# Rotated attention queries on all 128 partitions, padded with zeros

## The chip, the cores and the metric

The kernel runs on one core of one Trainium2 chip. The metric is the device time of one execution in microseconds (us); lower is better. TensorE (PE in the profile; PEld is its weight load, which can overlap the products) multiplies, VectorE (DVE) and ScalarE (ACT) work elementwise, GpSimd (POOL) here only fills tiles and copies a few columns, and SyncE (SP) issues most transfers.

## The reference

Two blocks of a network run over 256 tokens of width 2048, all in float32: gated linear attention with a convolution and a feed-forward, then a pooling mixer, then a multi-head attention layer. The change lies in the attention layer. It has 16 heads; the query and the key of a head have 192 values, of which 128 are plain and 64 are rotated by position. The rotated 64 of the key are the same for all heads up to a factor for each head and token.

```python
QBLOCK, N_HEADS, QK_NOPE, QK_ROPE, V_HEAD = 128, 16, 128, 64, 128
def qk_norm_rope(t, g, cos, sin):
    t = rmsnorm(t, g)
    return jnp.concatenate([t[..., :QK_NOPE], apply_rope(t[..., QK_NOPE:], cos, sin)], axis=-1)
def chunk_causal_attention(q, k, v):
    ...
    for i in range(S // QBLOCK):
        q0, k_end = i * QBLOCK, (i + 1) * QBLOCK
        s = jnp.einsum('bqhd,bkhd->bhqk', q[:, q0:k_end], k[:, :k_end]) * scale
        ...
        p = jax.nn.softmax(s, axis=-1)
        outs.append(jnp.einsum('bhqk,bkhd->bqhd', p, v[:, :k_end]))
```

## The kernel before

Activations lie transposed: features on the 128 partitions, 256 tokens along the row. All weights stream from HBM once, in the order of `weight_order`, in blocks of 1 MB. Each block is worked as two halves, called half-blocks here (a "unit" in the code). For each half-block ACT rounds the weights to a high part `wh` (L225), DVE takes the rest `wl` (L193), and PE multiplies both with the activations, which are split the same way. `wh` and `wl` have four buffers each and are made three half-blocks ahead, so ACT may run ahead of PE until it needs the buffer that PE still reads. PE executes strictly in the order in which the program was written.

Everything else is written as generators ("tasks") that take a step after a half-block: evictions from PSUM, norms, rotations, the attention itself. A task goes on when its tiles are there, when a PSUM place is free (three places called main, two called misc), and for attention when at least six of the 33 big tiles in SBUF ("slots") are free. So the number of live tiles helps to decide after which half-block a step is written, on all engines.

In the last stage the task `attend(hq)` does four heads at once (hq from 0 to 3; "head group" below). It writes the scores of two blocks of 128 queries. The first block sees 128 keys, the second 256; each is one main PSUM place of four heads. The heads stand in the order 0, 2, 1, 3. For each head there are two float32 products into the same place: the plain part, with queries `qn` and keys `kn` on 128 partitions, and the rotated part, with `qr` and `krp`. Two heads share a tile of rotated values: the even head has partitions 0 to 63 and the odd one 64 to 127, so this product takes 64 rows of the array. In the trace a float32 product is two passes, each a weight load (LDWEIGHTS) and a MATMUL; "64\*128" in a row is a product on 64 rows, "128\*128" one on 128.

Then ACT copies the scores to SBUF (`s`), POOL masks a corner, DVE takes the maximum, ACT the exponential, DVE divides, PE transposes (misc<-cm,s), ACT copies to `pt0` and `pt1`, PE multiplies with the values (main<-pt,v), ACT copies the result (`oraw`), DVE multiplies with the gate, and ACT and DVE split it into the `part` tiles that the output projection (bout, the last 32 half-blocks) reads, one head group after another. `qn_steps` also sums squares over partitions, as sixteen passes with a single column (misc<-ones,sq).

`qr_steps` makes the rotated queries, two tiles of eight heads, by `rope_rows`: a product with a fixed matrix, two multiplications with cosine and sine and one addition.

Of the kernel before, what the change touches and what calls it, by code (L numbers as in the profile page):

```python
# [99 lines left out]
def kernel(  # L100
# [11 lines left out]
    nc = tc.nc  # L112
# [36 lines left out]
    def slot(name, shape=(P, 4, T), dt=F32):  # L149
        return Slot(spool, big_places, "slot", shape, dt, name)  # L150
# [34 lines left out]
    def elems(a):  # L185
        return math.prod(a.shape[1:])
# [4 lines left out]
    def tt(out, a, b, op):  # L191
        vec_cost(out)
        nc.vector.tensor_tensor(out, a, b, op)  # L193

    def mul(out, a, b):
        tt(out, a, b, ALU.mult)

    def add(out, a, b):
        tt(out, a, b, ALU.add)
# [27 lines left out]
    def mm(out, lhsT, rhs, start, stop):  # L227
        n = elems(rhs)
        spent["PE"] += (n / 2.4 if rhs.dtype == F32R else max(n / 0.6, 214.0)) + 2
        nc.tensor.matmul(out, lhsT, rhs, start=start, stop=stop, skip_group_check=True)  # L230
# [188 lines left out]
    def group_tok(name, g, rhs, kbs=range(NKB)):  # L419

        ps = psum_now("main", (P, 2, 512))
        kbs = list(kbs)
        for i, kb in enumerate(kbs):
            for half in range(2):
                wh, wl = next_unit(name, g, kb)
                x = rhs(i)[half]
                for j in range(2):
                    first = i == 0 and half + j == 0
                    last = i == len(kbs) - 1 and half + j == 2
                    for t in range(2):  # L430
                        tk = slice(t * P, (t + 1) * P)
                        mm(ps[:, t, :], x[:, j, 0, tk], wh[:, j, :], first, False)
                        mm(ps[:, t, :], x[:, j, 0, tk], wl[:, j, :], False, False)
                        mm(ps[:, t, :], x[:, j, 1, tk], wh[:, j, :], False, last)
                end_unit()
        return ps
# [393 lines left out]
    for g in range(4):  # L830
        ps = group_tok("v", g, h)
# [4 lines left out]
    for g in range(4):  # L836
        hold = {}
        ps = group("cc", g, h)
# [6 lines left out]
        ps = group("cx", g, h)  # L845
# [19 lines left out]
        ps = group("cb", g, h)  # L865
# [12 lines left out]
    for g in range(4):  # L878
        ps = group("gb", g, h)
        gt = {}  # L880
        spawn(gate_steps(ps, get("R"), AF.Sigmoid, gt, 0))
        ps = group("conv_out", g, cbu)
# [11 lines left out]
    for g in range(4):  # L894
        ps = group("r", g, h)
# [15 lines left out]
    for g in range(4):  # L911
        ps = group("ga", g, h)
# [4 lines left out]
        ps = group("gla_out", g, op)  # L917
# [24 lines left out]
    def residual(g):  # L942
        def into(ps, fs):
            for part in range(2):
                add(xs[g][:, fs, :], ps[:, :, part, :], xs[g][:, fs, :])

        return into
# [77 lines left out]
    for part in range(4):  # L1025
# [5 lines left out]
        for g in range(4):  # L1031
            ps = group("down", g, hid, range(4 * part, 4 * part + 4), residual(g))
# [49 lines left out]
    for half in range(2):  # L1082
        y = Pair(4)
        for gi in (2 * half, 2 * half + 1):
            pooled = Pair(2)
            for n in range(2):
                ps = group("u", 2 * gi + n, hp)
# [5 lines left out]
            for n in range(2):  # L1093
                ps = group("pgate", 2 * gi + n, hp)
# [3 lines left out]
            for n in range(2):  # L1098
                ps = group("pgroup", 2 * gi + n, pooled, range(2))
# [15 lines left out]
        for g in range(4):  # L1115
            ps = group("pout", g, y, range(4 * half, 4 * half + 4), residual(g))
# [52 lines left out]
        yield from rms_steps(s, 512, r, cc)  # L1169
        rows["R" + key], rows["C" + key] = r, cc  # L1170

    def rope_rows(out, raw, n):

        ps = yield from psum_later("misc", (P, n, T))
        mm(ps.t, rot, raw, True, True)
        mul(out, raw, wide(C, n))
        yield 1
        t = slot("rt", (P, n, T))
        mul(t.t, ps.t, wide(S, n))
        ps.done()  # L1180
        add(out, out, t.t)
        t.free()

    kro = row("kro")
# [30 lines left out]
    kn, krp, vq = [None] * 4, [None] * 2, []  # L1215
# [42 lines left out]
        rk.free()  # L1258
        kn[g] = k

    qn, qr, qr2 = [None] * 4, [None] * 2, [None] * 2
    qss, qsc = small("qss", (P, 2, 16)), small("qsc", (P, 2, 16))

    def qn_steps(g, ps):
# [25 lines left out]
    def qr_steps(g, ps):  # L1290
        raw, sq = slot("qraw"), slot("sq")
        act(raw.t, ps.t, AF.Copy, scale=col("q_rope"))
        act(sq.t, ps.t, AF.Square)
        ps.done()
        qr2[g] = sq
        yield 2
        s = slot("qr")
        for b in range(2):
            yield from rope_rows(s[:, 2 * b:2 * b + 2, :], raw[:, 2 * b:2 * b + 2, :], 2)
        raw.free()  # L1300
        qr[g] = s

    ob = Pair(4)
    begun = {}
    HEAD_AT = (0, 2, 1, 3)
    def attend(hq):
        while None in (qn[hq], kn[hq], qr[hq // 2], krp[hq // 2]):
            yield 1
        while hq and (hq - 1 not in begun or state["unit"] < begun[hq - 1] + STAGGER):
            yield 1  # L1310
        while len(big_places) < 6:
            yield 1
        begun[hq] = state["unit"]

        rq = rows["Cq"]
        hs = slice(4 * hq, 4 * hq + 4)
        a, b = qss[:, :, hs], qsc[:, :, hs]
        for t in range(2):
            r = rq[:, t:t + 1]
            ts(qss[:, t, hs], qss[:, t, hs], r, r, ALU.mult, ALU.mult)  # L1320
        yield from rstd_steps(b, a, lambda: ts(a, a, 1.0 / QK_HEAD, EPS, ALU.mult, ALU.add))
        for t in range(2):
            ts(qsc[:, t, hs], qsc[:, t, hs], rq[:, t:t + 1], QK_HEAD**-0.5, ALU.mult, ALU.mult)
        probs, mxs = [], []
        for blk in range(2):
            w = P * (blk + 1)
            ps = yield from psum_later("main", (P, 4, T))
            qsl = slice(blk * P, (blk + 1) * P)
            for c in range(4):
                i = HEAD_AT[c]  # L1330
                hd = 4 * hq + i
                bs = slice(64 * (hd % 2), 64 * (hd % 2) + 64)
                jr = hd // 2
                mm(ps[:, c, 0:w], qn[hq][:, i, qsl], kn[hq][:, i, 0:w], c % 2 == 0, False)
                mm(ps[:, c, 0:w], qr[jr // 4][bs, jr % 4, qsl], krp[jr // 4][bs, jr % 4, 0:w], False, True)
            yield 1
            s = slot("s")
            probs.append(s)
            act(s[:, :, 0:w], ps[:, :, 0:w], AF.Copy)
            ps.done()  # L1340
            nc.gpsimd.memset(s[0:64, :, w - 64:w], -1e30)
        qn[hq].free()
        kn[hq].free()
        yield 1
        for blk in range(2):
            w = P * (blk + 1)
            mx = small("mx", (P, 3, 4))
            mxs.append(mx)
            nc.vector.reduce_max(mx[:, 0, :], probs[blk][:, :, 0:w], axis=AX.X)
            stt(mx[:, 0, :].rearrange("p (b a) -> p b a", b=2), mx[:, 0, :].rearrange("p (b a) -> p b a", b=2),  # L1350
                -1.0, qsc[:, blk, hs].rearrange("p (a b) -> p b a", b=2), ALU.mult, ALU.mult)
        yield 1
        for blk in range(2):
            w = P * (blk + 1)
            mx = mxs[blk]
            for c in range(4):
                hd = 4 * hq + HEAD_AT[c]
                sv = probs[blk][:, c, 0:w]
                act(sv, sv, AF.Exp, scale=qsc[:, blk, hd:hd + 1], bias=mx[:, 0, c:c + 1],
                    accum_out=mx[:, 1, c:c + 1])  # L1360
        yield 2
        for blk in range(2):
            w = P * (blk + 1)
            nc.vector.reciprocal(mxs[blk][:, 2, :], mxs[blk][:, 1, :])
            for c in range(4):
                sv = probs[blk][:, c, 0:w]
                ts(sv, sv, mxs[blk][:, 2, c:c + 1], None, ALU.mult)
        yield 2
        pt0, pt1 = slot("pt0"), slot("pt1", (P, 4, P))
        for src, sc, dst in ((probs[0], slice(0, P), pt0[:, :, 0:P]), (probs[1], slice(0, P), pt0[:, :, P:T]),  # L1370
                             (probs[1], slice(P, T), pt1.t)):
            ps = yield from psum_later("misc", (P, 4, P))
            for c in range(4):
                nc.tensor.transpose(ps[:, HEAD_AT[c], :], src[:, c, sc], ident)  # L1374
            yield 1
            act(dst, ps.t, AF.Copy)
            ps.done()
        for s in probs:
            s.free()
        yield 2  # L1380
        while len(vq) <= hq:
            yield 1
        po = yield from psum_later("main", (P, 4, T))
        for i in range(4):
            isl = slice(i * P, (i + 1) * P)
            mm(po[:, i, :], vq[hq][:, 0, isl], pt0[:, i, :], i % 2 == 0, False)
            mm(po[:, i, P:T], vq[hq][:, 1, isl], pt1[:, i, :], False, True)
        vq[hq].free()
        pt0.free()
        pt1.free()  # L1390
        yield 1
        o = slot("oraw")
        act(o.t, po.t, AF.Copy)
        po.done()
        while hq not in gates:
            yield 1
        yield 1
        mul(o.t, o.t, gates[hq].t)
        gates[hq].free()
        ob.put(hq, o.t)  # L1400
        o.free()
# [4 lines left out]
    for i, (name, g) in enumerate(MLA):  # L1406
# [8 lines left out]
        else:  # L1415
            ps = group_tok(name, g, cl, [0])
# [134 lines left out]
```

## Time and profile before

| | |
|---|---|
| three runs | 2775.38, 2773.48, 2775.07 us; median 2775.07 us |
| profiled execution, its own time | 2773.71 us |
| its span, first to last instruction | 2771.9 us |
| busy: PE, PEld | 2759.3 us (100%), 2403.6 us (87%) |
| busy: DVE, ACT, POOL | 1787.4 us (64%), 1346.4 us (49%), 25.7 us (1%) |
| mean granted TensorE clock | 0.999 of full speed |

Busy time of PE is not PE at its peak: matmuls are pipelined, and a product that waits inside the engine for its weights counts as busy. So the distance between starts tells more than a duration. A share of the whole span says little on the attention, which takes the last 210 us or so; stretches of it have to be asked for. The granted clock is given as a share of 2.4 GHz, so 0.50 is the lower of the two levels, 1.2 GHz.

### The profile page before, as it was taken

To read this page: it belongs to the slowest core of one execution; us is meant where nothing else is said; L and a number is where in the kernel's file an instruction comes from. 1 tells how busy PE (TensorE), PEld (TensorE's weight loads), DVE (VectorE), ACT (ScalarE), POOL (GpSimd) and SP (SyncE) were. 2 spreads that over 40 slices of the span, in tenths; PEclk is the share of its full clock that TensorE was granted. 3 is DMA by queue.
4 is the path that set the end of the run, shared out by engine and by line. 5 is a ranking of instruction groups with operands and counts; after the bars stand their busy time and mean duration, and the time that the engine had idled before them with its cause. 6 is when DMAs were issued, how large, how long until landed. Compare 5 with 4: busy or idle time off the path is not lost.

```text
span 2771.9 us, 38593 instructions
## 1 busy us (share of the span) xinstructions
PE 2759.3 (100%) x15906; PEld 2403.6 (87%) x15906; DVE 1787.4 (64%) x2119; ACT 1346.4 (49%) x1584; POOL 25.7 (1%) x36
## 2 busy tenths in 40 slices
PE   8999999999999999999999999999999999999999
PEld 7888888888888888888888888888888888899788
DVE  6676666655665666656556566687657677768464
ACT  5644444444554444434444345554434445555563
POOL 0000000000000000000000000000000000000000
PEclk9999999999999999999999999999999999999999
DMA  6444455555555655555555555555555555555244
GB/s 250 175 149 155 167 182 183 194 186 189 191 182 198 214 193 186 185 195 183 194 185 191 189 185 195 190 185 195 185 193 185 186 194 199 201 181 183 92 171 148
DMA packets 73712, 511.69 MB, mean 185 GB/s; under 512 B 8208, under 2 KB 8752, under 8 KB 13248
## 3 DMA queue, kind: packets, MB, share of 16 engines
q1 hardware_dynamic: 72496, 506.94, 51.9%
q8 instruction: 124, 2.03, 0.3%
q10 hardware_dynamic: 1040, 2.29, 0.2%
q14 instruction: 52, 0.43, 0.0%
HBM read 504.99 MB, written 4.21 MB: 184 GB/s over the span
## 4 chain that ended last, share of the span: by engine, by line
PE 99%; DVE 0%; DMA 0%; ACT 0%; issue 0%; SPq 0%; DVEq 0%; ACTq 0%
PE main L230 96%; PE misc L230 2%; DMA raw<-w_q_dram 0%; PE misc L1374 0%; DVE wl L193 0%; DVE cum L683 0%; ACT e L225 0%; ACT wh L225 0%; SPq L246 0%; ACT ls L225 0%; DVE x L193 0%; ACT L225 0%; DVE ls L206 0%; DVE out L193 0%; PE misc L1241 0%
## 5 line engine op out<-in xcount | busy, mean ns | idle before, releaser
L230 PE MATMUL main<-part,wh 128*128 128x512 f32 (+1 forms) x7360 | 2278.5, 392 | 6.9 <-ACT wh L225 6.9
L193 DVE TENSOR_TENSOR wl<-raw,wh 128x1024 fp32r<-128x1024 f32 (+1 forms) x946 | 1152.2, 1221 | 937.8 <-ACT wh L225 929.7
L230 PEld LDWEIGHTS main<-part,wl 128*128 128x128 f32 x7200 | 1354.4, 188 | 314.4 <-DVE wl L193 1.8
L225 ACT ACTIVATE wh<-raw 128x1024 fp32r<-128x1024 f32 (+1 forms) x946 | 997.3, 1058 | 1193.9 <-PE main L230 1100.1
L230 PE MATMUL main<-part,wl 128*128 128x256 f32 x7200 | 1430.2, 278 | 0.7 <-DVE wl L193 0.5
L230 PEld LDWEIGHTS main<-part,wh 128*128 128x128 f32 x7360 | 1124.0, 189 | 11.4 <-ACT wh L225 7.1
L193 DVE TENSOR_TENSOR out<-main,out 128x512 f32<-128x512 f32 x164 | 112.0, 684 | 8.3 <-ACT out L225 8.3
L230 PE MATMUL main<-wh,part 128*128 128x512 f32 x320 | 105.3, 400 | 0.0
L225 ACT ACTIVATE out<-main 128x512 f32<-128x512 f32 x164 | 94.6, 577 | 0.0
L193 DVE TENSOR_TENSOR x<-main,x 128x512 f32<-128x512 f32 x128 | 88.0, 688 | 9.9 <-PE main L230 7.7
L230 PEld LDWEIGHTS main<-wh,part 128*128 128x128 f32 x320 | 60.8, 190 | 12.8 <-issue 0.3
L230 PE MATMUL main<-wl,part 128*128 128x512 f32 x160 | 63.0, 394 | 0.0
L225 ACT ACTIVATE part<-out 128x512 fp32r<-128x512 f32 x56 | 33.2, 626 | 50.7 <-DVE out L206 44.2
L193 DVE TENSOR_TENSOR out<-out,R 128x1024 f32<-128x1024 f32 x42 | 51.4, 1225 | 1.3
L225 ACT ACTIVATE Z<-Z 128x1024 f32<-128x1024 f32 x16 | 17.0, 1061 | 42.0 <-DVE Z L193 36.9
L193 DVE TENSOR_TENSOR part<-out,part 128x512 fp32r<-128x512 f32 x56 | 36.2, 687 | 0.5
L230 PEld LDWEIGHTS main<-wl,part 128*128 128x128 f32 x160 | 30.6, 191 | 5.8
L225 ACT ACT_TABLE_LOAD x24 | 30.8, 1283 | 1.1 <-PEq L1540 0.7
L206 DVE SCALAR_TENSOR_TENSOR part<-x,vec,part 128x256 fp32r<-128x256 f32 x64 | 26.8, 478 | 5.3 <-ACT part L225 5.3
L1068 POOL COPY s<-out 128x4 f32<-128x4 f32 x8 | 9.5, 1187 | 2208.2 <-ACT wh L225 1809.7
L230 PEld LDWEIGHTS misc<-Z 128*128 128x128 f32 x240 | 29.0, 191 | 1.0
L230 PE MATMUL misc<-Z 128*128 128x64 f32 (+1 forms) x240 | 28.6, 271 | 0.0
(188 smaller groups left out, 824.4 us busy)
## 6 DMA issues: line engine op xcount, KB each, us to landing
raw<-w_up_dram SPq DMA_DIRECT2D x64, 1024.0 KB, 4.8
raw<-w_down_dram SPq DMA_DIRECT2D x64, 1024.0 KB, 4.8
raw<-w_u_dram SPq DMA_DIRECT2D x32, 1024.0 KB, 4.8
raw<-w_pgate_dram SPq DMA_DIRECT2D x32, 1024.0 KB, 4.8
raw<-w_pout_dram SPq DMA_DIRECT2D x32, 1024.0 KB, 4.8
raw<-w_v_dram SPq DMA_DIRECT2D x16, 1024.0 KB, 4.9
raw<-w_cc_dram SPq DMA_DIRECT2D x16, 1024.0 KB, 4.8
raw<-w_cx_dram SPq DMA_DIRECT2D x16, 1024.0 KB, 4.8
```

The lines of the kernel that those rows point to most:

```text
L193: nc.vector.tensor_tensor(out, a, b, op)
L206: nc.vector.scalar_tensor_tensor(out, a, s, b, op0, op1)
L225: nc.scalar.activation(out, a, f, bias=bias, scale=scale, **kw)
L230: nc.tensor.matmul(out, lhsT, rhs, start=start, stop=stop, skip_group_check=True)
L1068: nc.gpsimd.tensor_copy(nx[:, :, 0:d], cur[:, :, 0:d])
```

## The change

The rotated queries now get a tile of 128 partitions for each head group. POOL fills with zeros, for each head, the 64 partitions that the head doesn't have; `rope_rows` gets the target as `apart` and writes its last addition in two halves of 64 partitions to the places of the even and of the odd heads. The score product then takes all 128 partitions of `qr` and of `krp`, in which both heads of a pair lie; the other head's keys meet zeros. There are four `qr` tiles in place of two, and a scratch tile `rc`; each `qr` tile is freed with its head group's `qn` and `kn`.

```diff
-    def rope_rows(out, raw, n):
+    def rope_rows(out, raw, n, apart=None):
...
-        add(out, out, t.t)
+        if apart is None:
+            add(out, out, t.t)
+        else:
+            for b in range(2):
+                bs = slice(64 * b, 64 * b + 64)
+                add(apart[bs, b::2, :], out[bs], t[bs])
...
-        s = slot("qr")
+        s = slot("rc")
         for b in range(2):
-            yield from rope_rows(s[:, 2 * b:2 * b + 2, :], raw[:, 2 * b:2 * b + 2, :], 2)
+            z = slot("qr")
+            for a in range(2):
+                nc.gpsimd.memset(z[64 * a:64 * a + 64, 1 - a::2, :], 0.0)
+            yield from rope_rows(s[:, 2 * b:2 * b + 2, :], raw[:, 2 * b:2 * b + 2, :], 2, z)
+            qr[2 * g + b] = z
         raw.free()
-        qr[g] = s
+        s.free()
...
-        while None in (qn[hq], kn[hq], qr[hq // 2], krp[hq // 2]):
+        while None in (qn[hq], kn[hq], qr[hq], krp[hq // 2]):
...
-                mm(ps[:, c, 0:w], qr[jr // 4][bs, jr % 4, qsl], krp[jr // 4][bs, jr % 4, 0:w], False, True)
+                mm(ps[:, c, 0:w], qr[hq][:, i, qsl], krp[hq // 2][:, (4 * hq + i) // 2 % 4, 0:w], False, True)
...
-        qn[hq].free()
-        kn[hq].free()
+        for a in (qn, kn, qr):
+            a[hq].free()
```

The number of products stays: PE has as many instructions as before. Since other tiles are live, some steps stand after another half-block. Three places show it.

On DVE, where the first tile of rotated queries is made (`rc` scratch, `qr` target, `rt` the sine part, `wl` a half-block's weights):

```order
-L193 TENSOR_TENSOR qr_21071<-qraw_21005,C_19652 128x512
-L193 TENSOR_TENSOR wl_21104<-raw_20934,wh_21103 128x1024
-L193 TENSOR_TENSOR rt_21107<-misc_21072,S_19653 128x512
-L193 TENSOR_TENSOR qr_21071<-qr_21071,rt_21107 128x512
+L193 TENSOR_TENSOR rc_21071<-qraw_21005,C_19652 128x512
+L193 TENSOR_TENSOR wl_21107<-raw_20934,wh_21106 128x1024
+L193 TENSOR_TENSOR rt_21110<-misc_21075,S_19653 128x512
+L193 TENSOR_TENSOR qr_21072<-rc_21071,rt_21110 64x2x256 x2
```

One addition of 128 partitions becomes two of 64; the four tiles have it once each. The order around it is the same.

On ACT, the rows around the exponentials of head group 2 (names `s` with `mx`), where group 3's second block of scores is copied out of PSUM later on. Before:

```order
L225 ACTIVATE wh_21836<-raw_21581 128x1024
L225 ACTIVATE pt_2979_21750<-misc_21790 128x4x128
L225 ACTIVATE s_21685,mx_21805<-s_21685,mx_21805,qsc_20157 128x128 x4
L225 ACTIVATE s_21757,mx_21808<-s_21757,mx_21808,qsc_20157 128x256 x4
L225 ACTIVATE s_21856<-main_21814 128x1024
L225 ACTIVATE out_21688<-main_21646 128x512
```

And with the change:

```order
L225 ACTIVATE wh_21870<-raw_21656 128x1024
L225 ACTIVATE pt_2982_21748<-misc_21841 128x512
L225 ACT_TABLE_LOAD
L225 ACTIVATE s_21754,mx_21846<-s_21754,mx_21846,qsc_20157 128x128 x4
L225 ACTIVATE s_21809,mx_21849<-s_21809,mx_21849,qsc_20157 128x256 x4
L225 ACT_TABLE_LOAD
L225 ACTIVATE out_21681<-out_21681 128x1024
L225 ACTIVATE wh_21913<-raw_21656 128x1024
L225 ACTIVATE pt_3001_21875<-misc_21877 128x4x128
L225 ACTIVATE s_21925<-main_21890 128x1024
L225 ACTIVATE v_21928<-main_21821,Rl_20049 128x512 x2
```

`s_21856` and `s_21925` are the same copy, of the last block of scores. It stood right behind the exponentials; now a table load, a gate, a half-block's `wh` and a transposed block stand between. Over the whole program ACT has two table loads more.

On PE, the values of the last head group (main<-pt,v), the last half-block of the gate projection ahead of them (`part_19778`) and the first of the output projection. Before, where the rows of one half-block that only repeat are left out:

```order
L230 MATMUL main_22122<-part_19778,wh_22139 128x512 x2
L230 MATMUL main_22122<-part_19778,wl_22140 128x256 x2
L230 MATMUL main_22242<-pt_3033_22086,v_22013 128x256
L230 MATMUL main_22242<-pt_3034_22087,v_22013 128x128
...
L230 MATMUL main_22259<-part_22037,wh_22177 128x512 x2
L230 MATMUL main_22259<-part_22037,wl_22178 128x256 x2
```

And with the change:

```order
L230 MATMUL main_22124<-part_19778,wh_22141 128x512 x2
...
L230 MATMUL main_22259<-part_22036,wh_22181 128x512 x2
...
L230 MATMUL main_22260<-part_22036,wh_22207 128x512 x2
...
L230 MATMUL main_22313<-pt_3046_22155,v_22012 128x256
L230 MATMUL main_22313<-pt_3047_22156,v_22012 128x128
...
L230 MATMUL main_22259<-part_22148,wh_22244 128x512 x2
```

The values of the last head group are now multiplied behind the first two half-blocks of the output projection, and were ahead of both. Head groups 0 and 1 have their scores where they had them; the first scores of group 2 come two half-blocks later.

## Rows read from the trace of the kernel before

**Rows 1.** The page: shares of the chain that ended last, by engine.

```profile
PE 99%; DVE 0%; DMA 0%; ACT 0%; issue 0%; SPq 0%; DVEq 0%; ACTq 0%
```

**Rows 2.** A stretch: length, busy PE, PEld, DVE, ACT, POOL, granted clock, DMA.

```profile
2560.00:2630.00 70.00, 70.00 (x327) 50.77 (x326) 33.20 (x86) 38.08 (x80) 2.19 (x7) 0.95 0.25 89
```

**Rows 3.** Timeline of PE, group 2, first block: start, length, what, count.

```profile
2600.55 0.39 PE L230 MATMUL main<-kn,qn 128*128 128x128 f32 x2
...
2603.37 0.48 PE L230 MATMUL main<-krp,qr 64*128 64x128 f32 x2
2603.79 0.72 PE L230 MATMUL main<-part,wh 128*128 128x512 f32 x2
```

**Rows 4.** Timeline, group 1, second block, and a weight load in group 0.

```profile
2592.75 0.60 PE L230 MATMUL main<-kn,qn 128*128 128x256 f32 x2
2593.28 0.70 PE L230 MATMUL main<-krp,qr 64*128 64x256 f32 x2
...
2597.67 0.50 PE L230 MATMUL main<-part,wh 128*128 128x512 f32 x1
...
2576.96 0.29 PEld L230 LDWEIGHTS main<-krp,qr 64*128 64x128 f32 x2 [0.33 <-issue]
```

**Rows 5.** Timeline, products with the values of group 0, and what follows.

```profile
2641.44 2.81 PEld L230 LDWEIGHTS main<-pt,v 128*128 128x128 f32 x16
2641.66 2.78 PE L230 MATMUL main<-pt,v 128*128 128x256 f32 x16
2644.28 0.60 PE L1374 MATMUL misc<-cm,s 128*128 128x128 f32 x4
```

**Rows 6.** Timeline, single-column passes behind a half-block and behind scores.

```profile
2553.18 1.84 PE L230 MATMUL misc<-ones,sq 128*128 128x1 f32 x16
2554.89 0.47 PE L230 MATMUL main<-wh,part 128*128 128x512 f32 x1
...
2563.68 1.95 PE L230 MATMUL misc<-ones,sq 128*128 128x1 f32 x16
2565.49 0.49 PE L230 MATMUL main<-wh,part 128*128 128x512 f32 x1
```

**Rows 7.** Stretches around the two falls of the clock, columns as in rows 2.

```profile
2500.00:2566.50 66.50, 66.50 (x468) 60.74 (x467) 52.85 (x81) 38.37 (x42) 0.30 (x1) 1.00 0.54 184
2566.50:2570.20 3.70, 3.70 (x11) 2.92 (x10) 0.00 (x0) 0.43 (x2) 0.00 (x0) 0.56 0.58 244
2580.00:2584.00 4.00, 4.00 (x16) 3.49 (x15) 0.00 (x0) 0.48 (x1) 0.00 (x0) 0.58 0.01 4
```

**Rows 8.** Groups by shape (ACT: 2560 to 2690): count, busy, mean ns, idle before.

```profile
L193 DVE TENSOR_TENSOR qr<-qr,rt 128x512 f32<-128x512 f32 x4 | 2.8, 692 | 0.1
L193 DVE TENSOR_TENSOR krp<-sq,kro 64x512 f32<-64x512 f32 x8 | 5.5, 683 | 0.1
L706 POOL MEMSET ST<- 128x512 f32 x2 | 1.0, 524 | 0.0
L225 ACT ACT_TABLE_LOAD x6 | 7.7, 1283 | 0.1
L225 ACT ACTIVATE s<-s,mx,qsc 128x256 f32<-128x256 f32 x16 | 9.4, 587 | 0.0
L225 ACT ACTIVATE wh<-raw 128x1024 fp32r<-128x1024 f32 x27 | 28.4, 1055 | 24.1 <-PE main L230 18.6 <-issue 5.5
```

**Rows 9.** The chain in order of time: a transposition and a half-block.

```profile
2632.21 0.44 PE misc L1374 x4
2632.64 2.77 PE main L230 x12
```

**Rows 10.** Timeline behind the last group's values: half-blocks on PE, last part.

```profile
2677.49 0.70 PE L230 MATMUL main<-part,wh 128*128 128x512 f32 x2
2683.14 0.63 PE L230 MATMUL main<-part,wh 128*128 128x512 f32 x2
2686.64 1.29 DVE L193 TENSOR_TENSOR part<-oraw,part 128x512 fp32r<-128x512 f32 x2 [0.70 <-ACT part L225]
```

More of the change, by code (lines that the diff above doesn't have):

```diff
@@ L1259, in key_steps @@
         kn[g] = k
-    qn, qr, qr2 = [None] * 4, [None] * 2, [None] * 2
+    qn, qr, qr2 = [None] * 4, [None] * 4, [None] * 2
     qss, qsc = small("qss", (P, 2, 16)), small("qsc", (P, 2, 16))
@@ L1330, in attend @@
                 i = HEAD_AT[c]
-                hd = 4 * hq + i
-                bs = slice(64 * (hd % 2), 64 * (hd % 2) + 64)
-                jr = hd // 2
                 mm(ps[:, c, 0:w], qn[hq][:, i, qsl], kn[hq][:, i, 0:w], c % 2 == 0, False)
-                mm(ps[:, c, 0:w], qr[jr // 4][bs, jr % 4, qsl], krp[jr // 4][bs, jr % 4, 0:w], False, True)
+                mm(ps[:, c, 0:w], qr[hq][:, i, qsl], krp[hq // 2][:, (4 * hq + i) // 2 % 4, 0:w], False, True)
             yield 1
```

## The prediction

> **What bounds the kernel now.** I read the chain that ended last first: 99% of it is PE [rows 1]. So time is won only where PE itself gets shorter, and what DVE, ACT and POOL gain or lose counts only if PE comes to wait for them. Then I asked for the stretch of the scores, 2560 to 2630 us: PE is busy all of its 70.0 us, ACT 38.1, DVE 33.2, POOL 2.2, the transfers take a quarter of their engines, and the granted clock is 0.95 where it is 1.00 ahead of it [rows 2, 7]. Nothing makes PE wait there, but two things make it slow: the distance of the score products, and the clock. So the timeline of PE was next.
>
> A block of scores has eight products: four heads, plain and rotated in turn. Group 2's first block begins at 2600.55 and PE starts what follows at 2603.79, 3.24 us later; the last rotated product alone takes 0.42 from its start to the next one's [rows 3]. The second block, with 256 keys, takes 4.92 us [rows 4]. The nearest work on 128 rows is the product with the values: also float32, two passes each, weights loaded for each pass, eight products, half of them with 256 columns and half with 128, the two of a pair into one place. Those eight take 2.62 us, and their weight loads run in one piece that begins ahead of the first pass [rows 5]. In a block of scores the reader sees the reverse: the weight load sat idle for 0.33 us ahead of a pair and started when the pair before it had ended [rows 4].
>
> **The change, part by part.** *Score products.* A head group has a first and a second block, 16 products, of which half have 128 columns and half 256; that is twice what the values have. If on 128 rows they run at the distance of the values, a head group takes 2 x 2.62 = 5.24 us in place of 3.24 + 4.92 = 8.16, which is 2.92 less, and four groups 11.7 less. (The other six blocks are 3.22 to 3.24 and 4.91 to 4.92 long.) What follows a block pays too: the sixteen single-column passes take 1.71 us to the next start behind a half-block and 1.81 behind scores, so the first load behind a block of scores is late by 0.10 [rows 6]. Eight blocks, 0.8 us. Together 12.5 us; over 64 changes between 64 and 128 rows it is 0.195 us each. Bounds: nothing, if the distance has another reason (a rival below), and 12.5, since the products can't be closer than where loads are hidden. I take 12.5, because the values are equal in all but their rows.
>
> *Clock.* It stood at 0.56 over 3.70 us and at 0.58 over 4.00 us, and at 1.00 in the 66.5 us ahead [rows 7]. Lost: 3.70 x 0.44 + 4.00 x 0.42 = 1.63 + 1.68 = 3.3 us. Ahead of each fall PE did a block of scores and then the sixteen single-column passes; the same passes at 2553, behind a dense half-block, were followed by no fall, nor were the later blocks of scores that no such passes follow. With the change those two blocks become as dense as the products with the values, so what then stands ahead of the passes resembles 2553 more than 2563. Bounds: 0 if the passes alone are enough, 3.3 if both falls go. I take 3.3, with less trust than the first term.
>
> *DVE.* Four additions of 128 x 512 at 0.692 us become eight of 64 x 512, which have the time of `krp` at 0.683: +2.7 us [rows 8]. They lie ahead of 2560, where DVE is busy 52.9 of 66.5 us and PE never waits [rows 7]; each pair of additions sits behind the `wl` of a half-block that PE needs about two half-blocks later. Hidden; without the cover the next `wl` would be 0.7 us late, four times.
>
> *POOL.* Eight fills of 64 x 512. The trace has none; 128 x 512 takes 0.524 [rows 8], so between nothing and 0.524 each, 4.2 at most, on an engine busy for 2.2 us in 70. The additions wait for them, but each is written a half-block earlier. Nothing.
>
> *ACT.* Two more table loads at 1.283, 2.6 us [rows 8]. In the 130 us of the attention ACT idles 24.1 us ahead of `wh` alone, for the most part waiting for PE to free a buffer [rows 8]. Hidden, if no single place is tight. Two places are tighter than before.
>
> The first is the copy of group 3's second block out of PSUM: the values of group 0 go into that place next. On ACT sixteen instructions lead from the `wh` that waits for PE's buffer to this copy: two table loads, eight exponentials, five others of at most 1.06 (`wh`, gate, `wh`, a transposed block, the copy) and one more transposed block at half that. Taken high, 2.57 + 8 x 0.587 + 5.5 x 1.06 = 13.1 us. On PE, from that same buffer: three transpositions at 0.44, three half-blocks at 2.77 [rows 9] and the block of scores at twice the values' second half, 3.5: also 13.1. The exponentials are counted at their longer form and one transposed block at twice its time, so the true ACT sum is nearer 12.2, with about 1 us to spare. Nothing, but it can flip.
>
> The second is the tail: the last group's values come two half-blocks later, so four half-blocks remain until the seventh of the output projection needs them. A half-block there takes 2.8 us (two from 2677.49 to 2683.14), so 11.2. In the trace of before the last `part` was ready at 2687.93, 10.4 behind the end of the values at 2677.49, and that chain held a table load and a gate which the new order finishes earlier [rows 10]. Nothing.
>
> *Transfers.* No transfer is added; the loads of weights run a quarter of their engines' time here [rows 2].
>
> **The sum.** 12.5 + 3.3 = 15.8 us, off the profiled execution's own 2773.7 us (1.8 more than its span): 2757.9 us. The runs before had a median 1.4 higher and a lowest 0.2 lower; if that scatter is a fall of the clock more or less, it goes too, so I stay with 2758. A measurement of this kernel can tell about 0.2%, 5.5 us, from no change.
>
> **The rivals.**
>
> *The falls of the clock stay, one or both.* For it: the single-column passes hold PE at nearly no work for 1.7 us and stay [rows 6]; against it: 2553. One fall 2759.6, both 2761.2.
>
> *A wait takes part of the gain.* At group 3's copy, if ACT comes 1 us later than I count (a maximum that DVE delivers late ahead of the exponentials would do it), PE waits for the rest; the exponentials and table loads between would bound it at some 7 us. The tail could add a little, from 0.8 us of delay on. Time 2759 to 2765. For it: margins near 1 us; against it: ACT's 24 us of idleness and a PE that waited for no one in 70 us [rows 2, 8].
>
> *The rows are not the cost.* The 0.195 us might come from queries and keys themselves, whatever the rows. Then the change does nothing but add hidden work: 2773.7. Against it stand the products with the values [rows 5], which alternate tiles in the same way.
>
> *The other side: weight loads on 128 rows are not taken ahead.* If a load could overlap a running pass only where it fills other rows, then full rows would expose both loads of a product where now about one is. At 0.195 us for an exposed load, 64 products would pay 12.5 more: 2786.2. It decides from one exposed load per product on: fewer gain, more lose. The products with the values speak against it: sixteen exposed loads would add 3.1 us to passes that all fit in 2.62. The Trainium skill has this rule, in "TensorE: Matmul & The Clock Gate", Part 3, The mechanism: a weight load overlaps running products only when its row group differs. By that rule the result is the slow one just worked out; by this trace's rows on the values it does not hold for full-row products in a stream.
>
> **How the numbers follow.** Forecast as summed: 0.62, 2758.0, its own range 2756.5 to 2759.5. Falls of the clock stay: 0.17. A wait: 0.12. Rows are not the cost: 0.06. Loads exposed: 0.03. The range 2756 to 2765 takes in the first two and most of the third. Faster by over 0.2% (below 2769.5) is the first three less a bit: 0.90; within 0.2% 0.07; slower 0.03.
>
> **What would show it.** Right: eight products of a first block take about 1.75 us, of a second 3.5, all on 128*128; weight loads in one piece; the granted clock 1.00 through 2560 to 2630 and that stretch some 15.8 us shorter; PE still without waits. Clock wrong: 0.5 again behind the single-column passes. Sum wrong: a wait of PE's values on the copy of `s`, of the seventh output half-block on `part`, or score products still 0.4 us apart. A difference outside the attention would be none of this.

## The result and the profile after

| | before | with the change |
|---|---|---|
| four runs each, median (lowest to highest) | 2775.23 us (2773.48 to 2777.32) | 2760.55 us (2760.42 to 2761.18) |
| profiled execution, its own time; span | 2773.71; 2771.9 us | 2760.42; 2758.6 us |
| PE busy, DVE busy, ACT busy | 2759.3, 1787.4, 1346.4 us | 2744.5, 1789.3, 1348.8 us |

The ratio is 0.9948, with a 95% interval of 0.9933 to 0.9964: faster by half a per cent, inside the forecast range of 2756 to 2765 us. The profiled executions differ by 13.3 us; the sum had 15.8. So 2.5 us of the forecast gain did not arrive, and the profile says where 2.4 of them went.

The chain that ended last is no longer PE alone. Against [rows 1], ACT and DVE have a share of it. From the page of the changed kernel:

```profile
PE 97%; ACT 1%; DVE 1%; issue 0%; DMA 0%; SPq 0%; DVEq 0%; ACTq 0%
```

The stretches, in the columns of [rows 2]: length, busy PE, PEld, DVE, ACT, POOL, granted clock, DMA.

```profile
2560.00:2630.00 70.00, 70.00 (x410) 61.92 (x408) 39.47 (x100) 51.99 (x96) 2.45 (x8) 1.00 0.30 106
2630.00:2680.00 50.00, 47.59 (x284) 41.77 (x283) 32.58 (x45) 33.23 (x53) 0.00 (x0) 1.00 0.47 169
```

In the first one the granted clock is 1.00 where it was 0.95, and PE gets 410 instructions done where it did 327. In the second PE is busy for 47.59 of 50 us: 2.4 us of waiting, where it waited for no one before.

Head group 0 on PE, from the timeline (start, length, what, count):

```profile
2560.09 0.38 PE L230 MATMUL main<-kn,qn 128*128 128x128 f32 x2
...
2561.64 0.39 PE L230 MATMUL main<-krp,qr 128*128 128x128 f32 x2
2561.87 1.84 PE L230 MATMUL misc<-ones,sq 128*128 128x1 f32 x16
2563.57 0.49 PE L230 MATMUL main<-wh,part 128*128 128x512 f32 x1
...
2569.16 0.59 PE L230 MATMUL main<-kn,qn 128*128 128x256 f32 x2
...
2572.61 1.84 PE L230 MATMUL misc<-ones,sq 128*128 128x1 f32 x16
...
2579.99 0.39 PE L230 MATMUL main<-kn,qn 128*128 128x128 f32 x2
```

A first block takes 2561.87 - 2560.09 = 1.78 us, a second 3.45; before they took 3.24 and 4.92 [rows 3, 4]. The passes behind a block take 1.70 to the next start, as behind a half-block [rows 6]. In groups 1 to 3, where a half-block follows at once, the distances to its start are 1.70 and 3.27. Counted to the second start behind a block in groups 1 and 2, and over the passes in group 0, each block saves 1.55 to 1.57 us. The last row is the first block of group 1, 19.90 us behind that of group 0. The same two starts in the kernel before are 26.17 apart:

```profile
2560.46 0.38 PE L230 MATMUL main<-kn,qn 128*128 128x128 f32 x2
...
2586.63 0.38 PE L230 MATMUL main<-kn,qn 128*128 128x128 f32 x2
```

Between them stands the same work, so group 0 alone gave back 6.27 us. Of that 1.46 + 1.47 + 2 x 0.10 = 3.13 are its two blocks, a quarter of 12.5. The other 3.14 are the falls of the clock, which the forecast had at 3.3.

Now the 2.4 us of waits. What PE waited for from 2500 us on (waiting line, releaser, total, times, longest); the same view of the kernel before has no row at all:

```profile
PE misc L1380 <- ACT pt L225: 2.0, 2, 1.4
PE main L230 <- DVE out L193: 0.4, 1, 0.4
```

L1380 is a transposition. It needs one of the two misc places in PSUM, and ACT frees that place by its copy to `pt`. Neither of the prediction's two tight places is in this view. The copy of group 3's second block, the values that need its place, and the last `part` on DVE stand here:

```profile
2623.78 1.02 ACT L225 ACTIVATE s<-main 128x1024 f32<-128x1024 f32 x1
...
2625.66 2.78 PE L230 MATMUL main<-pt,v 128*128 128x256 f32 x16
...
2677.19 1.29 DVE L193 TENSOR_TENSOR part<-oraw,part 128x512 fp32r<-128x512 f32 x2 [0.70 <-ACT part L225]
```

The timeline shows how ACT came late at the misc places:

```profile
2631.29 1.28 ACT L225 ACT_TABLE_LOAD   x1 [1.30 <-DVE mx L206]
...
2636.86 1.24 ACT L225 ACTIVATE v<-main,Rl 128x512 f32<-128x512 f32 x2
...
2638.00 1.05 ACT L225 ACTIVATE wh<-raw 128x1024 fp32r<-128x1024 f32 x1
2639.08 1.23 DVE L193 TENSOR_TENSOR wl<-raw,wh 128x1024 fp32r<-128x1024 f32 x1 [5.41 <-ACT wh L225]
...
2640.22 1.22 DVE L193 TENSOR_TENSOR oraw<-oraw,out 128x1024 f32<-128x1024 f32 x1
...
2641.47 1.16 ACT L225 ACTIVATE part<-oraw 128x512 fp32r<-128x512 f32 x2 [2.42 <-DVE oraw L193]
...
2643.48 0.57 ACT L225 ACTIVATE pt<-misc 128x512 f32<-128x512 f32 x1
...
2644.20 0.63 PE L1380 MATMUL misc<-cm,s 128*128 128x128 f32 x4 [0.65 <-ACT pt L225]
...
2650.53 1.15 ACT L225 ACTIVATE part<-oraw 128x512 fp32r<-128x512 f32 x2 [3.19 <-DVE oraw L193]
...
2651.59 0.58 ACT L225 ACTIVATE pt<-misc 128x512 f32<-128x512 f32 x1
...
2652.22 0.66 PE L1380 MATMUL misc<-cm,s 128*128 128x128 f32 x4 [1.37 <-ACT pt L225]
```

Read it from below. `pt` stands on ACT behind `part`. `part` waits for DVE's `oraw`, which in the first case stands on DVE behind a `wl`. That `wl` waited 5.41 us for ACT's `wh`, which stood on ACT behind a table load, eight exponentials and two copies to `v`; and the table load had waited 1.30 for DVE's maximum. ACT and DVE hand the delay to each other, and two transpositions pay 0.65 and 1.37. How much of that the 1.30 alone makes is not shown.

### The profile page after: what moved, and what is told of

It is laid out like the page before. It is cut to its first block, busy times and chain, and to the rows that moved or that the text cites. A ratio compares the mean times of both kernels' runs of the same rounds, so it can differ in the third digit from the quotient of the medians.

```text
span 2758.6 us, 38606 instructions
## 1 busy us (share of the span) xinstructions
PE 2744.5 (99%) x15906; PEld 2401.9 (87%) x15906; DVE 1789.3 (65%) x2123; ACT 1348.8 (49%) x1586; POOL 29.9 (1%) x44
## 4 chain that ended last, share of the span: by engine, by line
PE 97%; ACT 1%; DVE 1%; issue 0%; DMA 0%; SPq 0%; DVEq 0%; ACTq 0%
PE main L230 95%; PE misc L230 2%; DMA raw<-w_q_dram 0%; ACT s L225 0%; DVE wl L193 0%; ACT wh L225 0%; ACT L225 0%; PE misc L1380 0%; DVE cum L683 0%; ACT v L225 0%; DVE oraw L193 0%; ACT e L225 0%; ACT pt L225 0%; DVE s L211 0%; ACT part L225 0%
## 5 line engine op out<-in xcount | busy, mean ns | idle before, releaser
L225 ACT ACTIVATE part<-x,vec 128x256 fp32r<-128x256 f32 x64 | 27.2, 494 | 2.9 <-DMA x<-xT 2.8
```

The source lines that it names most:

```text
L225: nc.scalar.activation(out, a, f, bias=bias, scale=scale, **kw)
```

## Experiments

Each kernel ran on the same chip as the kernel before, which had a median of 2773.78 us in the runs of the first four experiments and of 2774.01 in those of the last four. A ratio is that to the kernel before.

**The rows alone.** Everything of the change stays, tiles, fills, split additions and order; only the product goes back to the head's own 64 rows.

```diff
-mm(ps[:, c, 0:w], qr[hq][:, i, qsl], krp[hq // 2][:, (4 * hq + i) // 2 % 4, 0:w], False, True)
+bs = slice(64 * (i % 2), 64 * (i % 2) + 64)
+mm(ps[:, c, 0:w], qr[hq][bs, i, qsl], krp[hq // 2][bs, (4 * hq + i) // 2 % 4, 0:w], False, True)
```

> The changed kernel with its padded tiles, fills, slots and order, but the rotated product takes only the head's own 64 rows again. If the change between 64 and 128 rows is what the products paid for: eight products of a first block take 3.2 us again and of a second 4.9, so 12.5 us come back, the two falls of the clock (0 to 3.3) may come back, and PE's waits of 2.4 go because ACT has more time: 2770 to 2775 us. If the distance comes from the tiles and their layout and not from the rows: 2760.5 as with the change.

Measured: 2776.42 us (2774.63 to 2778.41), ratio 1.0007 (0.9997 to 1.0016), 1.4 above the expected range. The gain is gone, 15.9 us against the changed kernel. PE still waits, 0.9 us for a misc place and 0.4 for DVE, where the expectation had no waits left. Its timeline has the old distances back, and its clock falls again:

```profile
2560.35 0.48 PE L230 MATMUL main<-krp,qr 64*128 64x128 f32 x2
2560.77 0.49 PE L230 MATMUL main<-kn,qn 128*128 128x128 f32 x2
```

```profile
2565.00:2570.00 5.00, 5.00 (x17) 3.99 (x18) 0.17 (x1) 0.42 (x2) 0.00 (x0) 0.66 0.59 210
```

0.42 us from one start to the next, as in [rows 3], with tiles and order of the changed kernel. So the cost is in the change of rows, not in the tiles.

**The order alone.** The changed kernel, but attention goes on with five free slots in place of six. Then its steps stand behind the same half-blocks as before the change, and the two extra table loads are gone.

```diff
-        while len(big_places) < 6:
+        while len(big_places) < 5:
```

> The changed kernel, but attention may begin with five free slots instead of six; the head groups then stand where they stood before the change, and the two extra table loads are gone. If PE's 2.4 us of waits between 2642 and 2668 come from the later head groups: 2758.1 us, with those waits gone. If they come from PE being faster alone: 2760.5.

Measured: 2757.73 us (2757.24 to 2759.80), ratio 0.9941 (0.9927 to 0.9956). The profiled execution took 2758.04, which is 15.7 below that of the kernel before; the sum had 15.8. One of its four runs, the one of 2759.80, had a mean clock of 0.999, the others 1.000. The view of waits has no row for PE, and the second stretch is full:

```profile
2630.00:2680.00 50.00, 50.00 (x301) 44.37 (x300) 32.63 (x40) 31.75 (x42) 0.00 (x0) 1.00 0.51 184
```

So the waits came with the later head groups, and these came because the change holds more tiles, four `qr` and for a time `rc` where two `qr` were.

**No padding, products grouped.** The kernel before; in each block the four plain products come first and then the four rotated ones, on 64 rows as they were. That leaves two changes of rows in a block of eight.

```diff
             for c in range(4):
                 i = HEAD_AT[c]
+                mm(ps[:, c, 0:w], qn[hq][:, i, qsl], kn[hq][:, i, 0:w], c % 2 == 0, False)
+            for c in range(4):
+                hd = 4 * hq + HEAD_AT[c]
...
-                mm(ps[:, c, 0:w], qn[hq][:, i, qsl], kn[hq][:, i, 0:w], c % 2 == 0, False)
                 mm(ps[:, c, 0:w], qr[jr // 4][bs, jr % 4, qsl], krp[jr // 4][bs, jr % 4, 0:w], False, True)
```

> The kernel before, without padding, but each block of scores does its four plain products first and its four rotated ones behind them: two changes of rows for each block instead of eight. If a change of rows costs 0.195 us: 48 changes fewer, 9.4 us, and with or without the clock's 3.3: 2762 to 2766 us. If every product on 64 rows is slow by itself, the 32 rotated ones keep about 0.39 each: 2773 to 2775.

Measured: 2757.33 us (2756.45 to 2758.53), ratio 0.9939 (0.9924 to 0.9954), better than either theory expected. The rotated products are short:

```profile
2560.71 1.05 PE L230 MATMUL main<-kn,qn 128*128 128x128 f32 x8
2561.69 0.72 PE L230 MATMUL main<-krp,qr 64*128 64x128 f32 x8
2562.34 1.95 PE L230 MATMUL misc<-ones,sq 128*128 128x1 f32 x16
...
2571.34 1.89 PE L230 MATMUL main<-kn,qn 128*128 128x256 f32 x8
2573.16 1.14 PE L230 MATMUL main<-krp,qr 64*128 64x256 f32 x8
2574.23 1.95 PE L230 MATMUL misc<-ones,sq 128*128 128x1 f32 x16
```

From their first start to the next work four of them take 0.65 us with 128 keys and 1.07 with 256; in the changed kernel four products take half of 1.78 and of 3.45, so 0.89 and 1.73. A block is 1.63 and 2.89 us long, less than with full rows, although two changes are still in it. In this profile PE waits 0.3 us for ACT once, and one fall of the clock stays, behind the passes of group 0's first block:

```profile
2566.00:2567.00 1.00, 1.00 (x4) 0.73 (x3) 0.00 (x0) 0.75 (x2) 0.00 (x0) 0.50 0.56 188
```

**Halves in turn.** The same, but the rotated products alternate between the lower and the upper 64 partitions, where above two lower ones are followed by two upper ones.

```diff
-            for c in range(4):
+            for c in (0, 2, 1, 3):
                 hd = 4 * hq + HEAD_AT[c]
```

> As e3, but the four rotated products take the lower and the upper 64 partitions in turn, each into the other PSUM bank. If two products in different halves of the rows run beside each other, the rotated ones (10.5 us in all at 0.22 and 0.44 each) take half: 5.2 us less than e3, 2757 to 2761 us. If they only follow each other: as e3. If going from one half to the other costs as much as a change of rows, 3 more changes in each block than e3's one: up to 4.7 us more than e3.

Measured: 2757.41 us (2756.49 to 2760.28), ratio 0.9940 (0.9924 to 0.9957): the same. Four rotated products take 0.64 us with 128 keys (2561.46 to 2562.10). Turning more often neither helps nor costs. Whether products in different halves run beside each other is not settled by this pair, since both kernels use both halves; the next one does that.

**One half only.** The grouped kernel with all rotated products on partitions 0 to 63. The odd heads then take the even neighbour's data, so this kernel doesn't compute the rotated part of eight heads; its instructions are as many and as large.

```diff
-                bs = slice(64 * (hd % 2), 64 * (hd % 2) + 64)
+                bs = slice(0, 64)
```

> As e3 (plain products first, then the rotated ones), but all four rotated products take partitions 0 to 63; for the odd heads that is the neighbour's data, so half of the rotated parts are not the reference's. In e3 four rotated products took 0.65 us with 128 columns and 1.07 with 256, less than four at 0.22 and 0.44. If products in the two halves run beside each other: here 1.07 and 1.94, 1.3 us more for each head group, 2762.5 us. If a product on 64 rows is faster by itself: as e3, 2757.3.

Measured: 2762.22 us (2760.91 to 2762.75), ratio 0.9952 (0.9937 to 0.9967).

```profile
2560.54 1.16 PE L230 MATMUL main<-krp,qr 64*128 64x128 f32 x8
2561.63 1.95 PE L230 MATMUL misc<-ones,sq 128*128 128x1 f32 x16
...
2570.84 1.99 PE L230 MATMUL main<-krp,qr 64*128 64x256 f32 x8
2572.76 1.95 PE L230 MATMUL misc<-ones,sq 128*128 128x1 f32 x16
```

Four take 1.09 and 1.92 us here, 0.44 and 0.85 more than over two halves. From 128 to 256 keys they grow by 0.83, over two halves only by 0.42. So a product on 64 rows isn't shorter by itself: products on different halves run beside each other. Over four head groups 0.44 and 0.85 make 5.2 us, and the two medians differ by 4.9: this is why grouping gained more than expected. The Trainium skill says so in "TensorEngine Tiling (Array Packing)", Tiling Modes: different tiles can load weights and multiply in parallel. The two kernels agree with it.

**Which blocks the clock falls follow.** The changed kernel, with head group 0 on 64 rows; its two blocks are the ones that the single-column passes follow.

```diff
+bs = slice(64 * (i % 2), 64 * (i % 2) + 64) if hq == 0 else slice(0, P)
```

> The changed kernel, but head group 0, whose two blocks of scores stand ahead of single-column passes, takes 64 rows for the rotated products again. Two of eight blocks pay for 16 changes of rows: 3.1 us. If the falls of the clock belong to the slow blocks ahead of those passes, they come back too: 2764 to 2767 us and a clock of 0.5 in that place. If the falls have another cause: 2763.6 and no fall.

Measured: 2767.86 us (2765.25 to 2770.65), ratio 0.9974 (0.9963 to 0.9984), 0.9 above the range expected if the falls come back. The profiled execution is one of the longer runs, 2770.32. The first and the last of six stretches of one us, all at 0.50, and then the first starts of group 0 and of group 1:

```profile
2567.00:2568.00 1.00, 1.00 (x6) 1.00 (x6) 0.00 (x0) 0.30 (x1) 0.00 (x0) 0.50 0.71 131
...
2572.00:2573.00 1.00, 1.00 (x4) 0.81 (x3) 0.00 (x0) 0.00 (x0) 0.00 (x0) 0.50 0.00 0
```

```profile
2562.21 0.38 PE L230 MATMUL main<-kn,qn 128*128 128x128 f32 x2
...
2589.94 0.39 PE L230 MATMUL main<-kn,qn 128*128 128x128 f32 x2
```

27.73 us from group 0 to group 1, against 19.90 in the changed kernel. 3.13 of the 7.83 are the slower blocks, so its two falls cost 4.7 here. The first one lasted some 7 us, about twice as long as those of [rows 7].

**And the other half of it.** Group 0 alone on 128 rows, the three later groups on 64.

```diff
+bs = slice(64 * (i % 2), 64 * (i % 2) + 64) if hq > 0 else slice(0, P)
```

> The reverse: only head group 0 takes all 128 rows, groups 1 to 3 take 64 again. Six blocks pay for 48 changes of rows, 9.4 us, less some 1 to 2 us of waits that go because PE is slower: 2768 to 2770 us with no fall of the clock, if the falls belong to group 0; 3 us more, with falls, if they belong to the scores in general.

Measured: 2768.83 us (2768.44 to 2771.14), ratio 0.9980 (0.9971 to 0.9990). In the profile the clock stayed:

```profile
2560.00:2600.00 40.00, 40.00 (x221) 32.74 (x219) 19.43 (x49) 21.89 (x38) 1.22 (x4) 1.00 0.30 100
```

In these two profiles, with group 0 dense no fall comes although six slow blocks follow; with group 0 slow both come although six dense blocks follow. So the falls shown belong to group 0's blocks with the passes behind them, not to the passes alone. Seven of the ten runs with group 0 dense had a mean clock of 1.000; three had 0.999 and took 2770.3 to 2771.1 us, against 2768.4 to 2769.3 for the seven. No trace shows where the clock fell in those three.

**Four changes.** The kernel before, in pairs: two plain products, the two rotated ones of the same half, then the other half.

```diff
+            for cs in ((0, 1), (2, 3)):
+                for c in cs:
...
+                    mm(ps[:, c, 0:w], qn[hq][:, i, qsl], kn[hq][:, i, 0:w], c % 2 == 0, False)
+                for c in cs:
...
+                    mm(ps[:, c, 0:w], qr[jr // 4][bs, jr % 4, qsl], krp[jr // 4][bs, jr % 4, 0:w], False, True)
```

> The kernel before, but two plain products, then the two rotated ones of the same half, then the same for the other half: four changes of rows in a block, beside eight before and two in e3. At 0.195 us for a change, and products in one half one behind the other: 32 changes fewer, 6.2 us, about 2767.5 us. If 64-row products are faster by themselves and a change costs 0.25 to 0.3: about 2765.

Measured: 2765.91 us (2765.26 to 2767.54), ratio 0.9968 (0.9955 to 0.9981). The median lies between the two times expected, nearer to the rival's 2765, so the time doesn't decide; the profiled execution took 2767.54, and its rows do.

```profile
2560.46 0.60 PE L230 MATMUL main<-kn,qn 128*128 128x128 f32 x4
2560.99 0.71 PE L230 MATMUL main<-krp,qr 64*128 64x128 f32 x4
2561.63 0.71 PE L230 MATMUL main<-kn,qn 128*128 128x128 f32 x4
2562.27 0.71 PE L230 MATMUL main<-krp,qr 64*128 64x128 f32 x4
2562.91 2.64 PE L230 MATMUL misc<-ones,sq 128*128 128x1 f32 x16
2565.41 0.77 PE L230 MATMUL main<-wh,part 128*128 128x512 f32 x1
...
2573.51 1.02 PE L230 MATMUL main<-kn,qn 128*128 128x256 f32 x4
...
2577.64 1.95 PE L230 MATMUL misc<-ones,sq 128*128 128x1 f32 x16
```

The block is 2.45 us long; with eight changes it was 3.24 [rows 3]. Four changes are 0.79 us, 0.197 each, which is the forecast's 0.195 found by another way. Blocks with 256 keys give the same: 4.92 and 4.13. The rival's other premise, that a product on 64 rows is faster by itself, fell in the run on one half only.

## Why the prediction was right, and where its sum was off

The measured 2760.55 us lies in the stated range, but not in that of the forecast as summed, 2756.5 to 2759.5, which had a chance of 0.62. The range held because it took in the rival of a wait, which had 0.12. The cause and the size of the gain were right; that nothing would wait was not.

**Score products, 12.5 us: right.** The eight blocks took 1.70 to 1.78 and 3.27 to 3.45 us each; with what follows a block saved some 1.56, and eight times that are 12.5. That the changes of rows are the cost is shown three ways: by putting them back alone, by grouping, and by pairs. The rival that the rows are not the cost fell. The upper bound, that products can't be closer than where loads are hidden, holds for full rows only: the grouped kernel's blocks were shorter, 1.63 and 2.89.

**Clock, 3.3 us: right in size for the profiled execution; its reason only in part.** Between the first blocks of groups 0 and 1 it was worth 3.14. The argument by the passes at 2553 [rows 6] held as far as the passes go: the two experiments on group 0 turn the falls on and off by its blocks alone. All four runs of the changed kernel had a mean granted clock of 1.000. But the prediction gave the density of the blocks as the reason, and that is not shown: the grouped kernel's first block is shorter than the changed kernel's, 1.63 against 1.78 us, and the clock still fell to 0.50 behind it. In the profiles taken, every fall in this place came in a kernel whose group 0 has products on 64 rows. Padding doesn't rule a fall out either: one run in four of the second experiment and three in ten of the seventh had a mean clock of 0.999. How long a fall lasts also differs from run to run: among the later runs of the kernel before those with a mean clock of 0.999 took 2771.9 to 2774.1 us, and six with 0.997 took 2776.7 to 2777.5. So the term can be some 3 us more in other runs; that may be why the first experiment lost 15.9 us although its PE waited a little less. The rival that the falls stay fell for the changed kernel.

**DVE and POOL: right.** In the changed kernel, by shape (count, busy, mean ns, idle before):

```profile
L193 DVE TENSOR_TENSOR qr<-rc,rt 64x512 f32<-64x512 f32 x8 | 5.5, 686 | 0.2
L1306 POOL MEMSET qr<- 64x512 f32 x8 | 4.2, 523 | 293.4 <-PE misc L230 173.4 <-DVE krp L193 70.3 <-DVE part L206 31.1
L225 ACT ACT_TABLE_LOAD x26 | 33.4, 1283 | 4.0 <-DVE mx L206 2.9 <-PEq L1546 0.7
```

The additions are 686 ns long, the 683 of `krp`. A fill takes 523, the upper bound, since half the partitions save nothing; with the order of before (second experiment) all of it cost no time that shows.

**ACT: the step that failed.** The step read "Hidden, if no single place is tight", and then named two places. Neither made PE wait. The copy of group 3's second block ended at 2624.80 and the values that need its place began at 2625.66, so 0.9 us to spare where about 1 was forecast. The last `part` ended at 2678.48, 8.1 us behind the end of the values where 10.4 was taken, and delayed nothing. But there was a third place, some twenty us behind the first: two transpositions without a misc place, 2.0 us; and one product with values waited 0.4 for DVE. 2.4 us in all, which the sum had at nothing. The rival "a wait takes part of the gain" named one link of this chain in brackets, a maximum that comes late from DVE ahead of the exponentials (the 1.30 above), and gave it 0.12 and a time of 2759 to 2765; 2760.55 lies there. It looked for the wait in the wrong PSUM place. The second experiment shows the rest: with the old order this wait is gone, and the profiled execution, 2758.04 us, is 0.1 from the sum's 2757.9.

**Loads on 128 rows: the rival fell.** Full-row products of a block start 0.22 us apart with 128 columns; with both loads exposed it would have been (3.24 + 8 x 0.195) / 8 = 0.60. In its trace the two loads of the product at 2560.30 begin at 2560.20, while the product before, 0.38 us long from 2560.09, still runs. The Trainium skill, in "TensorE: Matmul & The Clock Gate", Part 3, The mechanism, has the rule behind this rival, that a weight load overlaps running products only when its row group differs; in this kernel's scores as in its values the trace does not agree with it for full-row products in a stream. What the Trainium skill says in "TensorEngine Tiling (Array Packing)", Tiling Modes, that a change of mode drains TensorE, the trace agrees with: at a change the load started about when the pair before it had ended [rows 4], and a change cost 0.195 to 0.197 us.

**What stays open.** The grouped kernel keeps one fall of the clock in two of its four runs (2758.5 and 2758.2 us, against 2756.5 in both others), so about 2 us. Whether another place of the single-column passes would remove that was not tried, and what in a block of group 0 makes the clock fall is open.

The fastest kernels are the grouped one without padding, 2757.33 us, the same with halves in turn, 2757.41, and the padded one with the order of before, 2757.73; their ranges overlap. The first needs no more memory, no fills and one edit of the loop.

## What to carry to other kernels

Count how often consecutive products change the number of rows they use, and write those of one kind together before padding them: grouping got all of the gain here without a tile more. Where a scheduler decides by free buffers, a change that holds more of them moves work far from the edit; compare the order of instructions, and follow each delayed instruction to the buffers that it frees, on every engine, not only those that looked tight first. A stretch of PE can also cost by a lower clock behind it, so look at the granted clock stretch by stretch.

## What the runs showed that was not expected

- Products on 64 rows in different halves run beside each other even when two of one half are written ahead of two of the other: 0.65 us for four in that order and 0.64 in turn, 1.09 in one half.
- The first fall of the clock to 0.50 lasted about 3.4 us in the profile of the kernel before and about 7 us in the kernel with group 0 on 64 rows and in the one with pairs. In these two the passes themselves were slowed: in the pairs kernel 2.50 us from their start to the next work at 2565.41, where the kernel before took 1.81.
- In the profiles of the grouped kernel and of the one with one half only, one fall came where the kernel before had two, behind the first block in one and behind the second in the other.
